# Products by seven in the down projection: fewer, later in their stages, and the turns before them on four banks

## Chip, cores and metric

The kernel runs on one core of one Trainium2 chip. The metric is the device time of an execution in microseconds; the time given for a kernel is the median of several runs. TensorE is called PE in the profile, VectorE DVE, ScalarE ACT, GpSimd POOL and SyncE SP.

## What is computed

One layer of an encoder for 256 tokens of width 2048 in float32. Attention in two kinds of windows comes first; then the gated MLP, which is where the change lies, and a gate by a second input:

```python
x = x + merged @ w_out[i]
hf = rms_norm(x, ffn_norm[i])
g = dwconv_centred(hf @ w_ffn_gate[i], conv_w[i], conv_b[i])
x = x + (jax.nn.gelu(g) * (hf @ w_ffn_up[i])) @ w_ffn_down[i]
gate_p = jax.nn.sigmoid(rms_norm(x, ple_norm[i]) @ w_ple_gate[i])
x = x + gate_p * (p[i] @ w_ple_proj[i])
...
return rms_norm(x, final_norm)
```

The MLP is 5632 wide (44 chunks of 128), with a convolution over three neighbouring tokens on the gate path.

## The kernel before

**Pieces.** All weights come from HBM as pieces of 128 x 2048 numbers (1 MB), in the order of use, into a ring of three buffers (`raw`, loads on SyncE's queue, L229). Each number is split into a high part (ScalarE, L249) and a low part (VectorE, L250). A product of two split operands is three matmuls (`thirds`, L350 to L352). The split units lie in a ring of six (`u`) and, for pieces by seven, a second ring of two (`v`), so VectorE and ScalarE can work ahead of TensorE by some three pieces.

**Plain pieces and pieces by seven.** In a `quad_stage` a piece holds two chunks of the contraction (a, b) by two column blocks of 512, and the tokens are two halves of 128. A plain piece (letter `s`) takes eight products, 24 matmuls of 512 columns, into the banks M2, M3, M4 and P22. A piece by seven (letter `S`) takes seven products, 21 matmuls, into M1, M7, M5, M6, M2, M3 and M4, by Winograd's form of Strassen's scheme. It asks for more elsewhere: VectorE forms differences of the weights in place (L242 to L244) and splits 3584 columns instead of 2048, and the moving side needs four sums of the activations of its two chunks, split too (`sums_of`, L821 to L827: four additions of 128 columns, a split of 512 on ScalarE and one on VectorE). Such a set of sums lies in one of five slots, tags 0 to 4. A set is made for a pair of chunks: pair 4 is chunks 8 and 9.

**Stages around the change.** The order is E0 to E5, F00, F01, E6 to E10, F10, F11, then pp0, pp1, G0, G2, G3. An E stage computes 512 columns of gate and of up for all tokens (8 pieces, pattern `ssssSsSs`). An F stage multiplies the activations of one half (24 or 20 chunks, so 12 or 10 pieces) with half of the columns of the down projection: F00 and F01 use groups 0 to 5, F10 and F11 groups 6 to 10. The letters of `DOWN` say which pieces of an F stage go by seven.

**What runs inside a stage.** Work on other engines is put at places (stage, piece, product) by `at` and issued when the loop gets there; the framework may still shift an instruction on its engine where its operands come late. At the start of a stage's last piece `row_sums` (L796 to L800) joins the banks of the products by seven: M1 by ScalarE, then M6, M7 and M5 on VectorE. As M2, M3, M4 and P22 end, `scaled` (L1021, L1022) finishes the rows of an E stage, and `residual` (L910 to L914) adds those of an F stage to the residual rows `xr`.

**Turns.** The rows of group g are turned to columns by TensorE in the next stage (`group_turns`, `turned`, L956: four transposes of 128 into a bank, copied out by ScalarE at L958): two calls for gate, two for up. The convolution and gelu (`mixer`, L965 to L973) and the product with up (`mixed`, L978 to L986) follow on VectorE and ScalarE, and `mixed` may make the set of sums at once (`held["early"]`). Sets that are not made there are made by `late` (L1016, then `sums_of`), which first adds the high and the low parts of the two chunks again. Four calls of `rows_pair` (L844, L447, L448) in F11 turn the first half of the new residual rows for the stage G0, and four more in pp0 the second half.

Of the kernel before, what the change touches and what calls it, by code (L numbers as in the profile page):

```python
# [90 lines left out]
NA = len(_JOBS)  # L91
ALT = "SsSsSsSs"
MLP = "ssssSsSs"
DOWN = ("SsSsSsSsSsss", "SsSsSsSsSs")
MLP_GROUPS = (range(0, 6), range(6, 11))
FIRST_GATES = "ssssSsSs"

# [1 line left out]
def _pieces():  # L99

    pieces, stages = [], {}

    def blocks(stage, items):
        stages[stage] = range(len(pieces), len(pieces) + len(items) // PIECE)
        for i in range(0, len(items), PIECE):
            pieces.append(("f", items[i:i + PIECE]))

    def quads(stage, n0, n1, pattern, k0=0):
        stages[stage] = range(len(pieces), len(pieces) + len(pattern))
        for i, c in enumerate(pattern):  # L110
            a, b = k0 + 2 * i, k0 + 2 * i + 1
            pieces.append((c, [(n0, a), (n1, a), (n1, b), (n0, b)]))

    def wide(stage, n, chunks):
        stages[stage] = range(len(pieces), len(pieces) + chunks // 4)
        for k in range(0, chunks, 4):
            pieces.append(("w", [(n, k + i) for i in range(4)]))

    a = [("w_in", k, j[2]) for k in range(KC) for j in _JOBS[:FIRST]]
    for _, _, n in _JOBS[FIRST:]:  # L120
        a += [("w_in", k, c) for k in range(KC) for c in (n if isinstance(n, tuple) else (n,))]
    blocks("A", a)
    for j in range(4):
        quads("B%d" % j, ("w_in", GA * P + j * WIDE), ("w_in", GB * P + j * WIDE), ALT if j else FIRST_GATES)
        wide("ba%d" % j, ("w_branch_a", j * WIDE), QH)
        wide("bb%d" % j, ("w_branch_b", j * WIDE), HG)
    for s in range(2):
        quads("D%d" % s, ("w_out", 2 * s * WIDE), ("w_out", (2 * s + 1) * WIDE), ALT)
    for half, groups in enumerate(MLP_GROUPS):
        for g in groups:  # L130
            quads("E%d" % g, ("w_ffn_gate", g * WIDE), ("w_ffn_up", g * WIDE), MLP)
        for s in range(2):
            quads("F%d%d" % (half, s), ("w_ffn_down", 2 * s * WIDE), ("w_ffn_down", (2 * s + 1) * WIDE),
                  DOWN[half], 4 * groups[0])
    for s in range(2):
        stages["pp%d" % s] = [len(pieces)]
        n0, n1 = ("w_ple_proj", 2 * s * WIDE), ("w_ple_proj", (2 * s + 1) * WIDE)
        pieces.append(("s", [(n0, 0), (n1, 0), (n1, 1), (n0, 1)]))
    quads("G0", ("w_ple_gate", 0), ("w_ple_gate", WIDE), ALT)
    for s in (2, 3):  # L140
        wide("G%d" % s, ("w_ple_gate", s * WIDE), KC)
    return pieces, stages


_PIECES, _STAGES = _pieces()
_NPIECES = len(_PIECES)

# [19 lines left out]
_LAST_OF = {u: o for u, o in _FBLOCKS}  # L167
_EARLY = [0] + list(np.cumsum([_LAST_OF[u] + 1 for u in range(40)]))
RINGS = {"u": 6, "v": 2}
HELD_TAGS = ({"act": (0, 1, 2, 3, 4), "next": (0, 1)}, {"act": (2, 3, 4, 0, 1), "next": (2, 3, 4, 0)})  # L170


@with_exitstack
def _encoder(ctx: ExitStack, tc, xt, pt, xrow, cols, gainrow, table, onehot, mask, ident_in, wts, out):
# [314 lines left out]
    due, rt, rc, held = {}, {}, {}, {}  # L489

    def at(i, f, *a):

        due.setdefault(i, []).append((f, a))
# [261 lines left out]
    for i, job in enumerate(_JOBS):  # L755
# [13 lines left out]
        if i == FIRST:  # L769
            for e in range(FIRST):  # L770
                late = max(e - KVH, 0)
# [38 lines left out]
    def quads(stage, moving, combos, finish):  # L810
        last = len(_STAGES[stage]) - 1
        row_sums(stage, last, finish)
        quad_stage(stage, moving, combos)
        run_due(stage, last, 8)
# [57 lines left out]
    for j in range(4):  # L872
# [15 lines left out]
        c = held["c"]  # L888
# [53 lines left out]
    mlp_pairs = [i for i, c in enumerate(MLP) if c == "S"]  # L942
# [7 lines left out]
    def turned(which, n, pair, c):  # L950

        p = bank(which, P, 2, T)
        for k in range(2):
            for t in range(2):
                first = n * WIDE + pair * T + k * P
                nc.tensor.transpose(p[:, k, t * P:(t + 1) * P], c[t][:, first:first + P], ident)  # L956
        u = held["tok"].tile([P, 2, T], F32, name="ut" if n else "gt", bufs=1 if n else 2)
        nc.scalar.activation(u, p, AF.Copy)  # L958
        return u

    def mixer(f, g):

        c = held["tok"].tile([P, 2, T], F32, name="cc")
        for k in range(2):
            nc.scalar.activation(c[:, k], g[:, k], AF.Identity, scale=tap(1, f + k), bias=tap(3, f + k))  # L965
            nc.vector.scalar_tensor_tensor(c[:, k, 1:], g[:, k, :-1], tap(0, f + k), c[:, k, 1:],
                                           op0=ALU.mult, op1=ALU.add)
            nc.vector.scalar_tensor_tensor(c[:, k, :-1], g[:, k, 1:], tap(2, f + k), c[:, k, :-1],
                                           op0=ALU.mult, op1=ALU.add)
        nc.scalar.activation(g, c, AF.Square, scale=math.sqrt(0.044715))  # L970
        nc.vector.scalar_tensor_tensor(g, g, 1.0, c, op0=ALU.add, op1=ALU.mult)
        nc.scalar.activation(g, g, AF.Tanh, scale=GELU_C)
        nc.vector.scalar_tensor_tensor(c, g, 1.0, c, op0=ALU.add, op1=ALU.mult)  # L973
        return c

    def mixed(k, c, u):

        nc.vector.scalar_tensor_tensor(u, u, 0.5, c, op0=ALU.mult, op1=ALU.mult)  # L978
        if 16 <= k < 20:
            for i in range(2):  # L980
                halves(activation_row(k + i), u[:, i])
        else:
            i = k // 20 * 2
            d = held["act"][i][:, k - 10 * i:k - 10 * i + 2]
            nc.scalar.activation(d[:, :, :T], u, AF.Copy)
            nc.vector.tensor_tensor(d[:, :, T:], u, d[:, :, :T].bitcast(F32), op=ALU.subtract)  # L986
        if k // 2 in held["early"]:
            combos["act", k // 2] = sums_of(u, held["early"][k // 2])

    def group_turns(half, g, down, c):  # L990

        k = 4 * (g - MLP_GROUPS[half][0])
        stage = "F%d0" % half if down else "E%d" % (g + 1)
        got = {}

        def gate(which, pair):
            got[pair] = turned(which, 0, pair, c)
            if pair == 0:
                got["c"] = mixer(4 * g, got[0])

        def up(which, pair):
            u = turned(which, 1, pair, c)
            mixed(k + 2 * pair, got["c"], u)
            if pair == 0:
                got["c"] = mixer(4 * g + 2, got[1])

        whens = ((0, 2), (0, 5), (1, 0), (1, 3)) if down else ((0, 3), (0, 6), (1, 1), (1, 5))
        for f, pair, which, when in zip((gate, gate, up, up), (0, 1, 0, 1), ("M1", "M5", "M6", "M7"), whens):
            at((stage, *when), f, "P22" if down else which, pair)

    def late(pair, tag):

# [19 lines left out]
        held["p"] = ph, pl  # L1032

    for half, groups in enumerate(MLP_GROUPS):
        pairs, tags = [i for i, c in enumerate(DOWN[half]) if c == "S"], HELD_TAGS[half]
        held["early"] = dict(zip(pairs, tags["act"][:3]))
        held["act"] = [big.tile([P, 16, 2 * T], FR, name="act", tag="R1"),
                       [big.tile([P, 2 * T], FR, name="act1", tag="yb%d" % i) for i in range(4)],
                       held["tok"].tile([P, 4, 2 * T], FR, name="act2")]
        for g in groups:  # L1040
            quads("E%d" % g, lambda k: hf[:, k, :], lambda i: combos["hf", i], scaled)
            group_turns(half, g, g == groups[-1], held["c"])
        for pair, tag in zip(pairs[3:], tags["act"][3:]):
            at(("F%d0" % half, pair - 4, 4), late, pair, tag)
        if half:
            at(("F10", 6, 0), load_last)
            at(("F10", 9, 0), split_last)
            held["ssq"] = sc.tile([P, 2, 2], F32, name="ssq", bufs=1)
        else:
            for pair, tag, when in zip(mlp_pairs, tags["next"], ((2, 4), (4, 4))):  # L1050
                at(("F01", *when), combine, "hf", hf, pair, tag)
        residual("F%d0" % half, 0, activation_row, "act", half)
        if half:
            pl = big.tile([P, KC, 2 * T], FR, name="pl", tag="R0")
            for pair, when in enumerate((("F11", 0, 6), ("F11", 1, 2), ("F11", 1, 5), ("F11", 2, 1))):
                at(when, rows_pair, "P22", pair, pl, 2)
            at(("F11", 2, 4), combine, "pl", pl, 0, tags["next"][0])
            at(("F11", 4, 4), combine, "pl", pl, 2, tags["next"][1])
        residual("F%d1" % half, 1, activation_row, "act", half)
# [52 lines left out]
    c = outputs()  # L1112
# [81 lines left out]
```

## Time and profile before

| what | value |
|---|---|
| median of 3 runs | 1469.82 us (1469.01 to 1470.96) |
| the profiled execution's own time | 1472.92 us |
| its span, first to last instruction | 1471.1 us |
| mean granted TensorE clock | 0.995 |
| ScalarE busy | 885.9 us (60%) |
| HBM read | 279.49 MB, 191 GB/s over the span |

Busy times are records that overlap on TensorE: the record of a matmul of 512 columns lasts 0.39 us, but the next one starts 0.23 later. So the space between starts is what counts there. In a row of a timeline the numbers are the start, the duration, the engine, the line, the operation and the tiles; in square brackets stands the idle time of the engine ahead of it and what ended that. In a row of a group, `x446 | 536.9, 1220 |` is the count, the busy time in us and the mean in ns.

### The profile page before, as it was taken

The page shows a single profiled execution, that of the slowest core. Times are in us where ns is not written, and L with a number is a line of the kernel's source. Part 1 is how long each engine was busy: PE and PEld are TensorE (multiplying, and loading weights), DVE is VectorE, ACT ScalarE, POOL GpSimd, SP SyncE. Part 2 cuts the span into 40 slices and gives each one's busy share as a digit, 9 for nine tenths or more (in the row PEclk, how much of TensorE's full clock was granted, in tenths as well). Part 3 has the DMA queues.
Part 4 walks back from the last instruction along what each step waited for, and adds up shares of the span by engine and source line. Part 5 has one row for each costly group of instructions (what it writes and reads, how often), then busy time and mean ns, then how long its engine had stood idle before and what let it go on. Part 6 is the DMA issues. An engine that isn't in the chain of part 4 may idle for free.

```text
span 1471.1 us, 18240 instructions
## 1 busy us (share of the span) xinstructions
PE 1449.0 (98%) x6892; PEld 1203.7 (82%) x6892; DVE 1292.3 (88%) x1720; ACT 885.9 (60%) x1188; POOL 4.9 (0%) x9
## 2 busy tenths in 40 slices
PE   9999999999999999999999999999999999989997
PEld 8888888888888888788888888788888878767786
DVE  7777764679998989999999999998899989999995
ACT  7555544445655655667666667554576766655663
POOL 0000000000000000000000000000000000000000
PEclk9999999999999999999999999999999999999998
DMA  9754445535555457454555444546535464345552
GB/s 324 256 203 143 168 163 183 175 120 208 217 188 212 172 200 273 163 193 176 225 200 200 170 174 172 216 185 246 211 136 203 177 228 173 145 157 218 200 206 111
DMA packets 46451, 282.80 MB, mean 192 GB/s; under 512 B 5076, under 2 KB 9812, under 8 KB 14108
## 3 DMA queue, kind: packets, MB, share of 16 engines
q1 hardware_dynamic: 45500, 280.46, 51.5%
q8 instruction: 54, 0.88, 0.2%
q10 hardware_dynamic: 864, 1.19, 0.2%
q14 instruction: 33, 0.27, 0.0%
HBM read 279.49 MB, written 2.14 MB: 191 GB/s over the span
## 4 chain that ended last, share of the span: by engine, by line
PE 88%; DVE 7%; ACT 2%; DMA 1%; issue 1%; POOL 0%; POOLq 0%; ACTq 0%; DVEq 0%
PE bank L351 22%; PE bank L352 22%; PE bank L350 22%; PE bank L293 7%; PE bank L300 4%; DVE ul L250 3%; PE bank L277 2%; PE bank L339 2%; PE bank L341 2%; PE bank L340 2%; DVE vl L250 1%; PE bank L956 1%; PE bank L278 1%; DMA raw<-in_wts 1%; ACT uh L249 1%
## 5 line engine op out<-in xcount | busy, mean ns | idle before, releaser
L249 ACT ACTIVATE uh<-raw 128x1024 fp32r<-128x1024 f32 (+2 forms) x518 | 507.5, 995 | 355.5 <-DMA raw<-in_wts 129.1
L250 DVE TENSOR_TENSOR ul<-raw,uh 128x1024 fp32r<-128x1024 f32 (+2 forms) x518 | 583.0, 1146 | 101.1 <-ACT uh L249 81.8
L350 PE MATMUL bank<-uh,hf 128*128 128x512 f32 x572 | 226.4, 396 | 0.6 <-DVE c L1021 0.6
L352 PE MATMUL bank<-uh,hf 128*128 128x512 f32 x572 | 223.3, 390 | 0.0
L351 PE MATMUL bank<-ul,hf 128*128 128x512 f32 x572 | 222.8, 389 | 0.0
L249 ACT ACTIVATE vh<-raw 128x1024 fp32r<-128x1024 f32 x136 | 143.1, 1056 | 59.1 <-DVE raw L242 33.2
L250 DVE TENSOR_TENSOR vl<-raw,vh 128x1024 fp32r<-128x1024 f32 x136 | 165.0, 1219 | 2.5 <-ACT vh L249 2.1
L352 PEld LDWEIGHTS bank<-uh,hf 128*128 128x128 f32 x572 | 107.3, 188 | 23.1
L350 PEld LDWEIGHTS bank<-uh,hf 128*128 128x128 f32 x572 | 107.4, 188 | 22.4 <-issue 1.3
L351 PEld LDWEIGHTS bank<-ul,hf 128*128 128x128 f32 x572 | 107.6, 188 | 21.2
L293 PE MATMUL bank<-hs,uh 128*128 128x512 f32 x432 | 103.6, 392 | 0.0
L350 PE MATMUL bank<-uh,act 128*128 128x512 f32 x232 | 89.9, 393 | 2.8 <-ACT uh L249 2.6
L293 PEld LDWEIGHTS bank<-hs,uh 128*128 128x128 f32 x432 | 79.5, 188 | 15.6
L351 PE MATMUL bank<-ul,act 128*128 128x512 f32 x232 | 90.5, 392 | 0.0
L352 PE MATMUL bank<-uh,act 128*128 128x512 f32 x232 | 90.1, 393 | 0.0
L350 PE MATMUL bank<-vh,S 128*128 128x512 f32 x204 | 79.7, 405 | 5.4 <-DVE c L797 3.1
L242 DVE TENSOR_TENSOR raw<-raw 128x1024 f32<-128x1024 f32 x68 | 82.9, 1220 | 0.5
L351 PE MATMUL bank<-vl,S 128*128 128x512 f32 x204 | 80.9, 396 | 0.6 <-DVE vl L250 0.6
L352 PE MATMUL bank<-vh,S 128*128 128x512 f32 x204 | 79.6, 393 | 0.0
L350 PE MATMUL bank<-uh,hs 128*128 128x512 f32 x172 | 67.3, 392 | 0.0
L352 PE MATMUL bank<-uh,hs 128*128 128x512 f32 x172 | 67.2, 391 | 0.0
L351 PE MATMUL bank<-ul,hs 128*128 128x512 f32 x172 | 67.1, 390 | 0.0
(254 smaller groups left out, 2565.7 us busy)
## 6 DMA issues: line engine op xcount, KB each, us to landing
raw<-in_wts SPq DMA_DIRECT2D x251, 1024.0 KB, 4.8
raw<-in_wts SPq DMA_DIRECT2D x12, 512.0 KB, 6.6
xr<-in_xrow SPq DMA_DIRECT2D x4, 512.0 KB, 8.1
x<-in_xt SPq DMA_DIRECT2D x13, 128.0 KB, 5.9
hb<-hold SPq DMA_DIRECT2D x3, 514.0 KB, 7.2
hb<-hold SPq DMA_DIRECT2D x2, 768.0 KB, 7.2
last<-in_gainrow SPq DMA_DIRECT2D x1, 1024.0 KB, 7.0
out<-xr SPq DMA_DIRECT2D x4, 256.0 KB, 2.6
```

The lines of the kernel that those rows point to most:

```text
L242: nc.vector.tensor_tensor(raw[:, :2 * WIDE], raw[:, WIDE:3 * WIDE], raw[:, :2 * WIDE], op=ALU.subtract)
L249: nc.scalar.activation(hi, src, AF.Copy)
L250: nc.vector.tensor_tensor(lo, src, hi.bitcast(F32), op=ALU.subtract)
L277: nc.tensor.matmul(acc, hi[:, w], m, start=first, stop=False, skip_group_check=True)
L293: nc.tensor.matmul(acc, weights(u)[0][:, o * P:(o + 1) * P], m, start=first, stop=False, skip_group_check=True)
L300: nc.tensor.matmul(acc[:, T:], weights(u)[1][:, o * P:(o + 1) * P], m[:, :T], start=False, stop=last, skip_group_check=True)
L339: nc.tensor.matmul(acc[:, :n * P], xh, hi, start=(k == 0), stop=False)
L340: nc.tensor.matmul(acc[:, :n * P], xh, lo, start=False, stop=False)
L341: nc.tensor.matmul(acc[:, :n * P], xl, hi, start=False, stop=(k == KC - 1))
L350: nc.tensor.matmul(acc, sh, wh, start=first, stop=False)
L351: nc.tensor.matmul(acc, sh, wl, start=False, stop=False)
L352: nc.tensor.matmul(acc, sl, wh, start=False, stop=last)
```

## The change

- `DOWN` has a pattern for each F stage: F00 four pieces by seven (pieces 4, 6, 8, 10), F01 five (0, 4, 6, 8, 10), F10 four (2, 4, 6, 8), F11 three (4, 6, 8). Before, each had five, at the even pieces from 0 to 8.
- The sets of sums of those pairs are made in `mixed`, where the activations arise. One set remains for `late`: pair 0 in half 0, made at piece 9 of F00 and used by F01's first piece. Slots and the two sets of `hf` made again in F01 move accordingly.
- The turns of a group stand at other places in the next stage: one or two products later in E stages, about three in F00, and in F10 at places of their own. Those of the last group of a half, which shared the bank P22, take M1, M5, M6 and M7 as the others do. So do the four turns of `rows_pair` in F11, at the places they had.

```diff
-DOWN = ("SsSsSsSsSsss", "SsSsSsSsSs")
+DOWN = (("ssssSsSsSsSs", "SsssSsSsSsSs"), ("ssSsSsSsSs", "ssssSsSsSs"))
...
-                  DOWN[half], 4 * groups[0])
+                  DOWN[half][s], 4 * groups[0])
...
-HELD_TAGS = ({"act": (0, 1, 2, 3, 4), "next": (0, 1)}, {"act": (2, 3, 4, 0, 1), "next": (2, 3, 4, 0)})
+HELD_TAGS = ({"act": {4: 0, 6: 1, 8: 2, 10: 3}, "next": (4, 0)},
+             {"act": {2: 1, 4: 2, 6: 3, 8: 4}, "next": (0, 1, 2, 3)})
...
-        whens = ((0, 2), (0, 5), (1, 0), (1, 3)) if down else ((0, 3), (0, 6), (1, 1), (1, 5))
+        whens = ((0, 5), (1, 0), (1, 3), (1, 6)) if stage != "F10" else ((0, 4), (0, 6), (1, 0), (1, 2))
         for f, pair, which, when in zip((gate, gate, up, up), (0, 1, 0, 1), ("M1", "M5", "M6", "M7"), whens):
-            at((stage, *when), f, "P22" if down else which, pair)
+            at((stage, *when), f, which, pair)
...
-        pairs, tags = [i for i, c in enumerate(DOWN[half]) if c == "S"], HELD_TAGS[half]
-        held["early"] = dict(zip(pairs, tags["act"][:3]))
+        tags = HELD_TAGS[half]
+        held["early"] = tags["act"]
...
-        for pair, tag in zip(pairs[3:], tags["act"][3:]):
-            at(("F%d0" % half, pair - 4, 4), late, pair, tag)
...
-            for pair, tag, when in zip(mlp_pairs, tags["next"], ((2, 4), (4, 4))):
+            at(("F00", 9, 4), late, 0, 4)
+            for pair, tag, when in zip(mlp_pairs, tags["next"], ((2, 4), (6, 4))):
                 at(("F01", *when), combine, "hf", hf, pair, tag)
...
-            for pair, when in enumerate((("F11", 0, 6), ("F11", 1, 2), ("F11", 1, 5), ("F11", 2, 1))):
-                at(when, rows_pair, "P22", pair, pl, 2)
+            for pair, (which, when) in enumerate((("M1", (0, 6)), ("M5", (1, 2)), ("M6", (1, 5)), ("M7", (2, 1)))):
+                at(("F11", *when), rows_pair, which, pair, pl, 2)
```

## Prediction

> **What bounds the kernel now.** I read the page first, then busy time by stage, then TensorE's rows where a stage is longer than its matmuls, then what VectorE and ScalarE did there.
>
> ```profile
> span 1471.1 us, 18240 instructions
> PE 1449.0 (98%) x6892; PEld 1203.7 (82%) x6892; DVE 1292.3 (88%) x1720; ACT 885.9 (60%) x1188; POOL 4.9 (0%) x9
> ```
>
> TensorE looks full, but matmul records overlap, so 98% hides short stalls. The table by stage shows them better. Its rows are, in order, E3, E5, F00, F01, E6, E10, F10, F11 and G0 (a stage runs from its first product to the next stage's first).
>
> ```profile
> core 0: us, PE busy (x) PEld busy (x) DVE busy (x) ACT busy (x) POOL busy (x), PEclk, DMA share, GB/s
> 761.34:806.18 44.84, 44.43 (x202) 36.51 (x203) 42.67 (x57) 31.24 (x42) 0.00 (x0) 1.00 0.52 189
> 850.28:894.37 44.09, 44.09 (x203) 36.47 (x202) 41.37 (x52) 30.62 (x42) 0.00 (x0) 1.00 0.45 161
> 894.37:961.82 67.45, 65.72 (x290) 51.86 (x289) 65.87 (x91) 43.39 (x56) 0.00 (x0) 1.00 0.49 186
> 961.82:1023.70 61.88, 61.88 (x274) 51.24 (x273) 58.34 (x70) 31.73 (x36) 0.00 (x0) 1.00 0.59 227
> 1023.70:1065.86 42.16, 42.16 (x187) 34.91 (x186) 34.15 (x36) 21.38 (x24) 0.00 (x0) 1.00 0.55 209
> 1198.91:1243.75 44.84, 44.43 (x202) 36.50 (x203) 42.12 (x52) 31.75 (x42) 0.00 (x0) 1.00 0.45 166
> 1243.75:1298.93 55.18, 54.48 (x243) 42.93 (x241) 54.82 (x81) 37.79 (x53) 0.00 (x0) 1.00 0.51 191
> 1298.93:1360.87 61.94, 56.50 (x238) 44.73 (x237) 58.93 (x77) 33.80 (x43) 0.00 (x0) 0.94 0.46 172
> 1373.64:1417.74 44.10, 42.38 (x185) 33.79 (x184) 42.98 (x61) 26.43 (x37) 1.07 (x1) 1.00 0.57 218
> ```
>
> A piece by seven products is 21 matmuls of 512 columns, a plain one 24. F01 holds 5x21 + 7x24 = 273 and no transposes, and took 61.88: 0.2267 us each. E6 confirms it (2x21 + 6x24 = 186; 42.16 / 186 = 0.2267). E5 has the same 186 and 16 transposes of a group's turns: 44.09 - 42.17 = 1.92, or 0.12 a transpose with its interruption. What exceeds this is stall:
> - F00: 67.45 - 61.88 - 1.92 = 3.65.
> - F10: 225 matmuls, 51.00; 55.18 - 51.00 - 1.92 = 2.26.
> - F11: 225 and 12 transposes; 61.94 - 51.00 - 1.44 = 9.50.
> - E3 and E10: 44.84 - 44.09 = 0.75 each.
> - G0: 180 matmuls and 4 transposes; 44.10 - 40.80 - 0.48 = 2.82.
>
> F00 and F10 are the stages where VectorE has no idle time (65.87 of 67.45, 54.82 of 55.18): it bounds them. F11 begins with what F10 left undone. Its first piece in TensorE's rows, then VectorE's:
>
> ```profile
> 1301.13 0.50 PE L350 MATMUL bank<-uh,act 128*128 128x512 f32 x1 [1.36 <-ACT uh L249]
> 1304.72 0.77 PE L350 MATMUL bank<-vh,S 128*128 128x512 f32 x1 [3.09 <-DVE c L797]
> 1305.29 0.63 PE L351 MATMUL bank<-vl,S 128*128 128x512 f32 x1
> 1305.71 0.63 PE L352 MATMUL bank<-vh,S 128*128 128x512 f32 x1
> ...
> 1309.55 0.55 PE L352 MATMUL bank<-uh,S 128*128 128x512 f32 x1
> 1309.94 0.39 PE L350 MATMUL bank<-uh,act 128*128 128x512 f32 x1
> ```
> ```profile
> 1301.63 1.22 DVE L250 TENSOR_TENSOR ul<-raw,uh 128x1024 fp32r<-128x1024 f32 x1
> 1302.76 1.21 DVE L250 TENSOR_TENSOR vl<-raw,vh 128x1024 fp32r<-128x1024 f32 x1
> 1303.90 0.68 DVE L797 TENSOR_TENSOR c<-bank,c 128x512 f32<-128x512 f32 x1
> 1304.50 0.67 DVE L910 TENSOR_TENSOR xr<-xr,bank 128x512 f32<-128x512 f32 x1
> ```
>
> F11 begins with a product by seven, which needs the banks M1, M7, M5 and M6 at once. They still hold F10's sums, whose first reader on VectorE (L797) stands behind weight splits and starts at 1303.90. TensorE waits 1.36 and 3.09. Then 11 matmuls come 0.43 apart instead of 0.23, at a granted clock that is 0.94 over the stage: 11 x 0.2 = 2.2 more. That is 7.4 of F11's 9.50 with the small gaps.
>
> [...]
>
> **The change part by part.**
>
> *Fewer pieces by seven.* 5+5+5+5 become 4+5+4+3. Four pieces go from 21 matmuls to 24: 12 x 0.2267 = +2.72 us on TensorE, certain: F00 276, F01 273, F10 228, F11 231. What each saves on VectorE comes from these groups:
>
> ```profile
> L250 DVE TENSOR_TENSOR ul<-raw,uh 128x1024 fp32r<-128x1024 f32 x446 | 536.9, 1220 | 84.3 <-ACT uh L249 65.8 <-PE bank L300 15.0 <-issue 1.9
> L250 DVE TENSOR_TENSOR vl<-raw,vh 128x1024 fp32r<-128x1024 f32 x136 | 165.0, 1219 | 2.5 <-ACT vh L249 2.1
> L242 DVE TENSOR_TENSOR raw<-raw 128x1024 f32<-128x1024 f32 x68 | 82.9, 1220 | 0.5
> L250 DVE TENSOR_TENSOR ul<-raw,uh 128x512 fp32r<-128x512 f32 x70 | 48.0, 686 | 12.3 <-ACT uh L249 11.4
> L243 DVE TENSOR_TENSOR raw<-raw 128x512 f32<-128x512 f32 x68 | 46.6, 685 | 0.5
> L244 DVE TENSOR_TENSOR raw<-raw 128x512 f32<-128x512 f32 x68 | 46.6, 685 | 0.4
> L827 DVE TENSOR_TENSOR S<-cmb,S 128x512 fp32r<-128x512 f32 x26 | 17.8, 684 | 0.1
> L821 DVE TENSOR_TENSOR cmb<-ut 128x128 f32<-128x128 f32 x26 | 7.4, 286 | 0.2
> L1016 DVE TENSOR_TENSOR ut<-act 128x256 f32<-128x256 f32 x8 | 3.2, 418 | 0.0
> ```
>
> By seven: 1.22 + 2 x 0.685 of differences, then splits 0.686 + 3 x 1.22. Plain: 2 x 1.22. The difference by durations is 4.5; the VectorE rows above start 1.13 and 0.60 apart, which makes it 4.1 of its time. A set of sums costs 0.684 + 4 x 0.286 = 1.8, and 2 x 0.42 more where it is made late: half 0 keeps five sets with one late instead of two, half 1 has four, none late, instead of five with two late. ScalarE, busy 43.39 of F00's 67.45, has room either way.
>
> Against TensorE's new need: F00 65.87 - 4.1 - 0.8 = 61.0 of 62.57 + 1.92 = 64.49 (95%, E5's share, which has no stall). F10, with about 5 us of its work that spilled into F11, needs some 60 now. It loses 4.1 and 2 x 0.84 + 1.8 = 3.5 of sums, since one of its two late sets is gone and the other is made at once: 52.4 of 53.60. That is full, but it enters with the weights of two pieces split ahead. F11 loses the spill and 2 x 4.1: 58.93 - 5 - 8.2 = 46 of 54.28. So I take the stalls of all three as gone: F00 64.49 (-2.96), F10 53.60 (-1.58), F11 54.28 (-7.66), the added matmuls included. What is late next is the bank M2, with which plain first pieces begin.
>
> *Turns placed later, on four banks.* E stages take them one or two products later (6 x 0.2267 = 1.36), F00 about three; F10 moves the first two later and the last one earlier.
>
> ```profile
> 1198.91 0.47 PE L350 MATMUL bank<-uh,hf 128*128 128x512 f32 x1 [0.55 <-DVE c L1021]
> 1201.75 0.55 PE L956 MATMUL bank<-ident,c 128*128 128x128 f32 x3 [0.41 <-ACT c L1022]
> 1371.27 1.15 PE L844 MATMUL bank<-ident,xr 128*128 128x128 f32 x9
> 1378.24 0.47 PE L350 MATMUL bank<-uh,pl 128*128 128x512 f32 x1 [0.79 <-DVE pl L448]
> ```
>
> In E10 the first turn waited 0.41 for scaled rows, 0.6 with the interrupted stream; E3 had the same. 1.36 later the rows are there: 2 x 0.6 = -1.2. In F00 and F10 the one bank cost little, since their 16 transposes show no long wait. In F11 the fourth pair's turn shares its bank with a running accumulation and slipped out of the stage: the 9 transposes at 1371 are part of 20 where four pairs need 16. On M7 it stays in F11: its 0.48 moves there (counted above), and G0 loses 0.48 and part of 2.82 of stall, one part of which is the 0.79 for L448. No row shows that cover, so between 0 and 2.82 I take 1.0, near the 0.79.
>
> *Sums made once, in the mixing.* ScalarE's split of a late sum stood in front of weights:
>
> ```profile
> 927.17 0.63 ACT L826 ACTIVATE S<-cmb 128x512 fp32r<-128x512 f32 x1 [5.11 <-DVE cmb L824]
> 930.81 0.73 PE L350 MATMUL bank<-uh,act 128*128 128x512 f32 x2 [1.21 <-ACT uh L249]
> ```
>
> That is F00's stall, counted already. New stalls: F11 and F00 begin plain and may wait for M2 as E10 did (0.55), and the one late sum left may hold ScalarE. Between 0 and 3.6 (F00's whole stall) I take +1.0, nearest the 0.55. The slots of the moved sets (tag 4 after E5, tag 0 after F01's fifth piece) are free pieces before their writers come, so I cost those waits at nothing; were one late, VectorE's weight splits queued behind it would pay. Pieces, their number and their loads on SyncE's queue stay as they are.
>
> **Sum.** -2.96 - 1.58 - 7.66 - 1.2 - 0.48 - 1.0 + 1.0 = -13.9. The profiled execution took 1472.92 (span 1471.1), so it would take 1459.0. The median of the runs, 1469.82, is 3.1 below it, and becomes 1455.9. A measurement tells some 0.2%, 2.9 us, from no change.
>
> **Rivals.**
> 1. *The stalls shrink only in part.* F10 stays full (52.4 of 53.60), so F11 starts late again. If 40% of 15.4 us of stalls stays, 6.2 is given back: 1462.1. For it: VectorE's need comes in lumps of a group's mixing. Against: F11 no longer asks for M1 first.
> 2. *The remaining late sum blocks ScalarE before F01*, as at 927: 3.6 back, 1459.5. [...]
> 3. *Slower: the later turns starve E stages.* VectorE idles 44.09 - 41.37 = 2.72 in E5. If the turns' 1.36 is lost for it and both following pieces by seven wait that long, each of the nine E stages with turns pays 2.72: 24.5 - 13.9 = +10.6, 1480. It decides from 13.9 / 9 = 1.5 a stage. Against: the idle time covers one such shift.
> 4. *The places do not bind.* The order on the engines is not the written one (the slipped turn shows it); if the turns run where they ran, the 1.2, 0.48 and 1.0 stay: 1458.6.
>
> **How the numbers follow.** Forecast 60%, rival 1 17%, rival 2 7%, rival 4 9%, rival 3 7%. The range goes from 1453.0 (all of G0's 2.82 and no new stall: 1.8 and 1.0 less) to 1462.0, rival 1. Faster by over 0.2% takes all but rival 3 and the worst of rival 1: 0.89; same 0.05; slower 0.06.
>
> **What would show it.** Right: F00 near 64.5, F10 53.6, F11 54.3 with a clock of 1.00, no wait on L797 over 1 us, E3 and E10 at 44.1, all 16 turns of the first four pairs in F11. Wrong: F stages over these by more than 2 us, E stages above 45, or VectorE idle in E5 over 3 us while TensorE waits on its splits.

## The result, and the profile after

The changed kernel takes 1460.01 us (median of 6 runs, 1459.24 to 1460.69). The kernel before took 1470.94 in the 6 runs beside it (1469.01 to 1471.51). The ratio is 0.9929, with a 95% interval from 0.9916 to 0.9941: 10.9 us faster. The forecast time was 1455.9, with a range from 1453.0 to 1462.0. The profiled execution took 1460.40, with a span of 1458.6.

The table of stages, with the columns shown before, has these rows for the changed kernel: E3, F00, F01, E10, F10, F11 and G0.

```profile
core 0: us, PE busy (x) PEld busy (x) DVE busy (x) ACT busy (x) POOL busy (x), PEclk, DMA share, GB/s
762.33:806.49 44.16, 44.16 (x203) 36.49 (x203) 41.79 (x56) 30.51 (x41) 0.00 (x0) 1.00 0.52 191
894.88:960.50 65.62, 65.01 (x294) 53.22 (x292) 62.31 (x82) 43.81 (x56) 0.00 (x0) 1.00 0.49 179
960.50:1022.70 62.20, 62.20 (x275) 51.15 (x273) 59.37 (x73) 32.86 (x36) 0.00 (x0) 1.00 0.62 229
1197.66:1242.83 45.17, 44.36 (x202) 36.40 (x203) 41.70 (x56) 30.14 (x42) 0.00 (x0) 1.00 0.50 187
1242.83:1296.95 54.12, 54.05 (x245) 44.29 (x245) 53.97 (x72) 37.69 (x51) 0.00 (x0) 1.00 0.52 199
1296.95:1351.25 54.30, 54.30 (x249) 44.87 (x247) 52.02 (x69) 31.57 (x42) 0.00 (x0) 1.00 0.55 199
1364.04:1405.24 41.20, 41.20 (x181) 33.53 (x180) 40.47 (x56) 24.48 (x30) 1.07 (x1) 1.00 0.64 241
```

F11 is now as long as TensorE's records in it (54.30 of 54.30), at a clock of 1.00. F00 and F10 came down too; they are 1.1 and 0.5 us longer than their matmuls and turns. G0 gave 2.9 us, and nothing in it was edited. From E1 to F11, TensorE's rows hold four waits of more than 0.15 us. Three are for the bank M2, at the first product of E3 (0.45), E10 (0.38) and F10 (0.81); the fourth is in F00's seventh piece, for a weight split. The two longest:

```profile
1242.83 0.47 PE L351 MATMUL bank<-uh,act 128*128 128x512 f32 x1 [0.81 <-DVE c L1022]
...
932.03 0.50 PE L352 MATMUL bank<-vl,S 128*128 128x512 f32 x1 [0.61 <-DVE vl L251]
```

(Lines of the changed kernel stand one later: L1021 is L1022, L250 is L251.)

| stretch | before | after | difference | predicted |
|---|---|---|---|---|
| E1 to E5 and E7 to E10 | 399.35 | 399.33 | 0.0 | -1.2 |
| F00 | 67.45 | 65.62 | -1.8 | -3.0 |
| F01 | 61.88 | 62.20 | +0.3 | 0 |
| F10 | 55.18 | 54.12 | -1.1 | -1.6 |
| F11 | 61.94 | 54.30 | -7.6 | -7.7 |
| pp0, pp1, G0 | 56.87 | 53.99 | -2.9 | -1.5 |
| new stalls, in no stage | | | | +1.0 |

(A wait for a stage's first product is counted to the stage before it, so F10's 0.81 is in E10.) The rows add up to -13.1. The spans differ by 12.5, since stages ahead of E1 took 0.6 longer, which the edit does not touch.

### The profile page after: what moved, and what is told of

The parts are those of the page before. It is cut to its first block, busy times and chain, and to the rows that moved or that the text cites. A ratio compares the mean times of both kernels' runs of the same rounds, so it can differ in the third digit from the quotient of the medians.

```text
span 1458.6 us, 18224 instructions
## 1 busy us (share of the span) xinstructions
PE 1444.6 (99%) x6904; PEld 1205.6 (83%) x6904; DVE 1273.4 (87%) x1689; ACT 880.7 (60%) x1179; POOL 4.8 (0%) x9
## 4 chain that ended last, share of the span: by engine, by line
PE 83%; DVE 11%; DMA 2%; issue 2%; ACT 2%; POOLq 0%; POOL 0%; DVEq 0%; SPq 0%; ACTq 0%
PE bank L351 21%; PE bank L353 20%; PE bank L352 20%; PE bank L294 7%; DVE ul L251 4%; PE bank L301 4%; DMA raw<-in_wts 2%; PE bank L340 2%; PE bank L342 2%; PE bank L341 2%; PE bank L278 2%; DVE vl L251 1%; PE bank L279 1%; DVE raw L243 1%; PE bank L845 1%
## 5 line engine op out<-in xcount | busy, mean ns | idle before, releaser
L250 ACT ACTIVATE uh<-raw 128x1024 fp32r<-128x1024 f32 (+2 forms) x518 | 507.8, 999 | 346.7 <-DMA raw<-in_wts 119.7
L251 DVE TENSOR_TENSOR ul<-raw,uh 128x1024 fp32r<-128x1024 f32 (+2 forms) x518 | 584.0, 1149 | 100.0 <-ACT uh L250 80.9
L250 ACT ACTIVATE vh<-raw 128x1024 fp32r<-128x1024 f32 x128 | 134.5, 1057 | 65.6 <-DVE raw L243 29.4
L251 DVE TENSOR_TENSOR vl<-raw,vh 128x1024 fp32r<-128x1024 f32 x128 | 155.0, 1218 | 0.9 <-ACT vh L250 0.5
L351 PE MATMUL bank<-uh,act 128*128 128x512 f32 x256 | 100.9, 394 | 0.8 <-DVE c L1022 0.8
L353 PE MATMUL bank<-uh,act 128*128 128x512 f32 x256 | 100.0, 391 | 0.0
L352 PE MATMUL bank<-ul,act 128*128 128x512 f32 x256 | 99.7, 389 | 0.0
L243 DVE TENSOR_TENSOR raw<-raw 128x1024 f32<-128x1024 f32 x64 | 78.0, 1219 | 0.6
L352 PE MATMUL bank<-vl,S 128*128 128x512 f32 x192 | 75.4, 392 | 0.6 <-DVE vl L251 0.6
L351 PE MATMUL bank<-vh,S 128*128 128x512 f32 x192 | 75.7, 398 | 0.1
L353 PE MATMUL bank<-vh,S 128*128 128x512 f32 x192 | 74.3, 390 | 0.0
```

The costliest lines, as they stand in the source:

```text
L243: nc.vector.tensor_tensor(raw[:, :2 * WIDE], raw[:, WIDE:3 * WIDE], raw[:, :2 * WIDE], op=ALU.subtract)
L250: nc.scalar.activation(hi, src, AF.Copy)
L251: nc.vector.tensor_tensor(lo, src, hi.bitcast(F32), op=ALU.subtract)
L351: nc.tensor.matmul(acc, sh, wh, start=first, stop=False)
L352: nc.tensor.matmul(acc, sh, wl, start=False, stop=False)
L353: nc.tensor.matmul(acc, sl, wh, start=False, stop=last)
```

## The experiments

The notation is as in the diff above. Each kernel ran in turn with the kernel before, as a rule five times (ten times in experiment 2, four times for the second kernel of experiment 9).

**1. F11 alone, in the kernel before.** The first two experiments ask why F11 stalled for 9.5 us.

```diff
-DOWN = ("SsSsSsSsSsss", "SsSsSsSsSs")
+DOWN = (("SsSsSsSsSsss",) * 2, ("SsSsSsSsSs", "ssssSsSsSs"))
...
-            for pair, when in enumerate((("F11", 0, 6), ("F11", 1, 2), ("F11", 1, 5), ("F11", 2, 1))):
-                at(when, rows_pair, "P22", pair, pl, 2)
+            for pair, (which, when) in enumerate((("M1", (0, 6)), ("M5", (1, 2)), ("M6", (1, 5)), ("M7", (2, 1)))):
+                at(("F11", *when), rows_pair, which, pair, pl, 2)
```

> The kernel before, in which F11 alone begins with four plain pieces (three by seven instead of five) and turns its four pairs on M1, M5, M6 and M7. F00, F01 and F10 stay as before, so F10 leaves as much VectorE work undone as before. Theory A (F11's 9.5 us of stall are F10's undone VectorE work): the undone work stays, F11's first products wait for M2 in place of M1, F11 is 58 us or more, and the time 1465 or more. Theory B (the stall is that a piece by seven asks for M1, M7, M5 and M6 at once): F11 is near 54.3, G0 near 41.2 as in the changed kernel, and the time 1460 to 1462. F10 stays near 55.2 in both.

It took 1464.38 us, 0.9963 of before (0.9950 to 0.9975). The stages F10, F11 and G0, and TensorE's row between the first two:

```profile
1241.17:1299.22 58.05, 54.72 (x243) 42.72 (x241) 57.77 (x84) 37.98 (x52) 0.00 (x0) 1.00 0.51 194
1299.22:1354.38 55.16, 54.68 (x247) 44.93 (x248) 51.37 (x68) 31.66 (x42) 0.00 (x0) 1.00 0.55 200
1367.87:1409.24 41.37, 41.21 (x182) 33.69 (x181) 40.64 (x56) 24.39 (x30) 1.07 (x1) 1.00 0.66 249
```
```profile
1299.22 0.50 PE L350 MATMUL bank<-uh,act 128*128 128x512 f32 x1 [2.63 <-DVE xr L910]
```

The wait of 2.63 ends with F11's first product, so the table counts it to F10. It is the undone work of theory A: M2, in place of M1, comes free late. But it is one wait instead of two, and the clock stays at 1.00. With the wait F11 is 57.8, just under theory A's 58, and the time is just under its 1465; without it F11 is 55.2, and G0 is where theory B has it. So the truth lies between the two.

**2. F11 alone as before, in the changed kernel.**

```diff
-        ... ("ssSsSsSsSs", "ssssSsSsSs"))
+        ... ("ssSsSsSsSs", "SsSsSsSsSs"))
...
+            at(("F10", 5, 4), late, 0, 0)
...
-            ... ((("M1", (0, 6)), ("M5", (1, 2)), ("M6", (1, 5)), ("M7", (2, 1)))):
+            ... ((("P22", (0, 6)), ("P22", (1, 2)), ("P22", (1, 5)), ("P22", (2, 1)))):
```

> The changed kernel with F11 as before: five pieces by seven from its first piece on, turns on P22; the sums of pair 0 are made late in F10. Theory A (undone work of F10, which is now gone): F11 is 51.0 of matmuls + 1.4 of turns + at most 1.5 of waiting, 54 or less, with a clock of 1.00; with 2.9 given back in G0 for the slipped turn the time is about 1462.5. Theory B (the form with which F11 begins): a wait on L798 of 3 us or more, a slower clock and F11 of 58 to 62, so a time of 1467 to 1470.

It took 1467.79 us, 0.9978 of before (0.9969 to 0.9987). F10, F11 and G0, and the first waits in F11:

```profile
1243.15:1297.36 54.21, 54.12 (x244) 44.18 (x245) 54.17 (x77) 38.67 (x53) 0.00 (x0) 1.00 0.47 180
1297.36:1354.80 57.44, 54.15 (x239) 42.95 (x238) 56.82 (x75) 32.75 (x42) 0.00 (x0) 1.00 0.49 184
1367.53:1411.64 44.11, 42.52 (x186) 33.76 (x185) 43.26 (x62) 26.80 (x37) 1.06 (x1) 1.00 0.57 222
```
```profile
1299.36 0.50 PE L351 MATMUL bank<-uh,act 128*128 128x512 f32 x1 [1.16 <-ACT uh L250]
1301.01 0.50 PE L351 MATMUL bank<-vh,S 128*128 128x512 f32 x1 [1.15 <-DVE c L798]
```

The two waits are those of before, 1.36 and 3.09, made smaller. F10 and F11 together took 117.12 before, 113.21 in the first experiment, 111.65 here and 108.42 in the changed kernel. Relieving F10 is worth 4.8 to 5.5 us, and beginning F11 plainly, with two pieces by seven fewer, 3.2 to 3.9. Neither theory holds alone: theory B's time came, but not its wait of 3 us or its slower clock. The shares add up, and F10's is the greater.

**3. The fourth turn on P22 again.**

```diff
-            ... ("M6", (1, 5)), ("M7", (2, 1)))):
+            ... ("M6", (1, 5)), ("P22", (2, 1)))):
```

> The changed kernel with one edit: the fourth turn of the residual rows in F11 is put on P22 again. Theory: the turn slips out of F11 as before, F11 loses 0.5 us, G0 goes from 41.2 back towards 44.1, and the time is 1462.4. Rival: G0 became shorter because VectorE arrives there with less undone work, and the turn does not matter: G0 stays under 42 and the time at 1460.0.

It took 1460.71 us, 0.9930 of before (0.9918 to 0.9942), which cannot be told from the changed kernel. F11, then pp0 with pp1, then G0, and the last turns:

```profile
1295.26:1349.07 53.81, 53.81 (x245) 44.48 (x244) 50.93 (x67) 30.58 (x40) 0.00 (x0) 1.00 0.55 198
1349.07:1362.77 13.70, 13.56 (x69) 10.82 (x68) 13.49 (x20) 13.07 (x25) 0.00 (x0) 1.00 0.28 98
1362.77:1404.10 41.33, 41.20 (x181) 33.68 (x180) 40.60 (x56) 24.46 (x31) 1.07 (x1) 1.00 0.62 245
```
```profile
1357.69 1.58 PE L845 MATMUL bank<-ident,xr 128*128 128x128 f32 x13
```

The turn did slip: its transposes come after F11, among the 13 at 1357.69. G0 stays short all the same. The slip costs 0.4 net (13.70 against 12.79, and F11 0.49 less). So the slip of this turn is not what G0's gain comes from, and the rival stands.

**4. Four pieces by seven in F11.**

```diff
-        ... ("ssSsSsSsSs", "ssssSsSsSs"))
+        ... ("ssSsSsSsSs", "ssSsSsSsSs"))
...
-            ... ((("M1", (0, 6)), ("M5", (1, 2)), ("M6", (1, 5)), ("M7", (2, 1)))):
+            ... ((("M1", (0, 6)), ("M5", (1, 0)), ("M6", (1, 2)), ("M7", (1, 5)))):
```

> The changed kernel with four pieces by seven in F11 (2, 4, 6, 8) instead of three, and its turns up to one product earlier. TensorE needs 0.7 us less, VectorE 4.1 more. Theory (what VectorE saves in F11 is spent on working ahead, and shortens G0): G0 goes from 41.2 to 42.5 or more, the time stays at 1460 to 1462. Rival (F11 has room for it, as predicted by its 46 of 54 us): F11 53.6, G0 41.2, time 1459.3.

It took 1460.20 us, 0.9931 of before (0.9919 to 0.9943). F11 and G0:

```profile
1296.89:1350.60 53.71, 53.71 (x245) 44.29 (x244) 53.21 (x71) 32.59 (x43) 0.00 (x0) 1.00 0.51 189
1363.40:1405.05 41.65, 41.52 (x181) 33.49 (x180) 40.84 (x59) 25.10 (x34) 1.07 (x1) 1.00 0.61 230
```

F11 gains 0.6, as the rival had it, G0 loses 0.45, and the time stays. G0's 41.65 is under the 42.5 that the theory set, but goes its way a little. VectorE's busy time rose by 1.2 in F11, not by the 4.1 that the added piece asks for, so it did less of something else there. Over the kernels shown, busy times of 50.93 to 53.21 in F11 go with 41.20 to 41.65 in G0, though not in order; the second experiment's 56.82 and the 58.93 of before go with 44.11 and 44.10. That fits an engine that spends what it need not do in F11 on working ahead for G0. It is argued, not shown: no run varies that lead by itself, and both kernels with the long G0 also turn all four pairs in F11 on P22.

**5. The E stages' turns at their old places.**

```diff
+        if stage[0] == "E":
+            whens = ((0, 3), (0, 6), (1, 1), (1, 5))
```

> The changed kernel with the turns in the E stages at the places of before; F00 and F10 keep the new ones. Theory (the later turns save the waits for scaled rows in two stages): 1461.2, with the sum of E1 to E5 and E7 to E10 1.2 us longer. Rival (the places only move the waits from one stage to another): 1460.0 within 0.4. Second rival (the later turns cost VectorE time): 1459.0 or less.

It took 1461.69 us, 0.9937 of before (0.9923 to 0.9950), an interval that overlaps the changed kernel's. E3, E9 and E10, and E3's wait (in this kernel L1022 is L1025):

```profile
761.92:806.76 44.84, 44.43 (x203) 36.52 (x203) 42.69 (x57) 31.10 (x42) 0.00 (x0) 1.00 0.52 188
1153.96:1198.06 44.10, 44.10 (x204) 36.48 (x203) 41.16 (x55) 29.43 (x40) 0.00 (x0) 1.00 0.51 187
1198.06:1242.73 44.67, 44.37 (x204) 36.44 (x203) 41.76 (x56) 30.26 (x41) 0.00 (x0) 1.00 0.52 191
```
```profile
764.76 0.55 PE L957 MATMUL bank<-ident,c 128*128 128x128 f32 x3 [0.41 <-ACT c L1025]
```

The 0.41 in E3 comes back, so the later place does remove it. But E10 is 0.5 shorter than in the changed kernel, and the nine E stages take 398.80, where the theory had them 1.2 longer than the changed kernel's 399.33. The gain of a stage is lost in another, as the first rival has it. The rival's time did not come: the median is 1.7 over the changed kernel's. In the profile the excess lies outside the E stages (pp0 with pp1 takes 14.29 for 12.79), and whether it means anything, the intervals do not say.

**6. Two sets of sums made late again.**

```diff
-HELD_TAGS = ({"act": {4: 0, 6: 1, 8: 2, 10: 3}, ...
-             {"act": {2: 1, 4: 2, 6: 3, 8: 4}, ...
+HELD_TAGS = ({"act": {4: 0, 6: 1, 8: 2}, ...
+             {"act": {2: 1, 4: 2, 6: 3}, ...
...
+            at(("F10", 4, 4), late, 8, 4)
...
+            at(("F00", 6, 4), late, 10, 3)
```

> The changed kernel with two of its sets of sums made late again: pair 10 at the seventh piece of F00 and pair 8 at the fifth piece of F10. Each costs VectorE 0.84 us more, and a split on ScalarE that waits for VectorE. Theory (VectorE and ScalarE are full in F00 and F10, so a late set is paid for by TensorE): F00 and F10 1 to 2 us longer each, 1462 to 1464. Rival (it costs no more than can be hidden): 1460.0 within 0.5.

It took 1461.83 us, 0.9938 of before (0.9925 to 0.9950): 1 to 2 us over the changed kernel, within what the intervals leave open. F00 and F10 are not longer (65.07 and 54.11); F01 is 63.24 and F11 55.10, 1.0 and 0.8 over the changed kernel. F01's is one wait, in its first piece:

```profile
961.68 0.47 PE L351 MATMUL bank<-vh,S 128*128 128x512 f32 x1 [1.07 <-DVE c L798]
```

If the sets have a price, it shows a stage later than the theory put it.

**7. Five pieces by seven in F00.**

```diff
-DOWN = (("ssssSsSsSsSs", ...
+DOWN = (("ssSsSsSsSsSs", ...
...
+        if stage == "F00":
+            whens = ((0, 4), (0, 6), (1, 0), (1, 2))
...
+        if not half:
+            at(("E5", 7, 4), late, 2, 4)
         for g in groups:
```

> The changed kernel with five pieces by seven in F00 (pieces 2, 4, 6, 8, 10) instead of four; the sums of pair 2 are made late, at the end of E5; F00's turns stand where F10 has them. TensorE needs 0.7 us less, VectorE 6.7 more (4.1 for the piece, 2.6 for the set). Theory (the number of pieces by seven bounds F00 through VectorE): F00 67 or more, time 1461.5 to 1464. Rival (that they begin after two plain pieces is what counts): F00 65 and time 1459.3.

It took 1465.56 us, 0.9955 of before (0.9942 to 0.9969): 5.5 slower than the changed kernel. Four of the five executions took 1464.31 to 1465.91 at a mean granted clock of 0.996 or 0.997, the fifth 1461.97 at 0.998. F00 and F01, and F01's start:

```profile
893.92:959.04 65.12, 64.25 (x290) 52.69 (x290) 63.22 (x87) 43.04 (x57) 0.00 (x0) 1.00 0.48 178
959.04:1025.62 66.58, 64.01 (x275) 52.35 (x273) 63.64 (x77) 34.52 (x38) 0.00 (x0) 0.97 0.59 215
```
```profile
960.71 0.50 PE L351 MATMUL bank<-vh,S 128*128 128x512 f32 x1 [0.84 <-ACT vh L250]
962.95 0.80 PE L352 MATMUL bank<-vl,S 128*128 128x512 f32 x1 [1.74 <-DVE vl L251]
963.54 0.63 PE L353 MATMUL bank<-vh,S 128*128 128x512 f32 x1
963.97 0.63 PE L351 MATMUL bank<-vh,S 128*128 128x512 f32 x1
```

The median is 1.6 over the theory's range, and the loss is not where the theory put it. F00 itself is 0.5 shorter, as the rival had it, and F01 pays 4.4, with a slow clock again (0.97 over the stage). F01 was not edited. Late pieces alone do not help: with five of them the debt is paid where the next stage begins by seven. This is how F10 and F11 stood to each other before. The edit does three things, and no run separates the piece, its set made late and the places of the turns.

**8. F01 like F00, with no late set at all.**

```diff
-        ... "SsssSsSsSsSs"), ...
+        ... "ssssSsSsSsSs"), ...
...
-            at(("F00", 9, 4), late, 0, 4)
```

> The changed kernel with F01 as F00 (four pieces by seven, the first at piece 4), so that the late set of pair 0 is gone. TensorE needs 0.7 us more in F01. Theory (F00's wait of 0.8 at its piece 6 is for the late set, which VectorE takes there already): F00 from 65.6 to 64.6, F01's 0.3 gone, together 0.6 less: 1459.4. Rival (the wait has another cause): F00 65.6 and the time 1460.5.

It took 1459.88 us, 0.9926 of before (0.9913 to 0.9938): no different from the changed kernel. F00 is 65.95, and its wait of 0.6 in the seventh piece is still there, so the late set is not its cause. F01 is 63.25, of which its 276 matmuls take 62.57, so F01's 0.3 did not go either. Rows of the changed kernel ahead of F00's wait suggest another cause. They are VectorE's and SyncE's (with what SyncE waited for from 905 to 921 us, in total, times and longest), then ScalarE's and VectorE's:

```profile
918.40 1.22 DVE L251 TENSOR_TENSOR vl<-raw,vh 128x1024 fp32r<-128x1024 f32 x1
919.65 0.33 SPq L230 DMA_DIRECT2D raw<-in_wts  x1
```
```profile
SPq L230 <- DVE vl L251: 14.8, 1, 14.8
```
```profile
925.65 1.06 ACT L250 ACTIVATE uh<-raw 128x1024 fp32r<-128x1024 f32 x1 [4.76 <-DMA raw<-in_wts]
```
```profile
926.74 1.22 DVE L251 TENSOR_TENSOR ul<-raw,uh 128x1024 fp32r<-128x1024 f32 x1 [0.97 <-ACT uh L250]
```

SyncE had waited 14.8 us for a buffer of the ring of three, until VectorE, with rows of the mixing between its splits, had read it out at 919.62. The load then came late, ScalarE and VectorE idled for it, and the split that TensorE wanted stood behind that piece's. So the late load is VectorE's lag again, by way of the buffers. This is read from the rows; no run varies the buffers, so it stays open.

**9. More pieces by seven where VectorE has time: E6.** E6 has no turns, and VectorE worked 34 of its 42 us.

```diff
-            quads("E%d" % g, ..., MLP)
+            quads("E%d" % g, ..., MLP if g != 6 else "ssSsSsSs")
...
+            at(("F01", 8, 4), combine, "hf", hf, 2, 1)
```

> The changed kernel with one piece by seven more in E6 (2, 4, 6 instead of 4, 6); the sums of its pair are made in F01. E6 has no turns, and VectorE is busy 34 of its 42 us. TensorE needs 0.7 us less, VectorE 4.1 + 2.4 more. Theory (an added piece by seven is free where VectorE has idle time, and only there): E6 41.5 without waits, E7 unchanged, 0.7 less than the changed kernel. Rival (the debt appears in E7, as F10's does in F11): E6 41.5, but E7 0.5 to 2 longer, and the time the same or longer.

The second kernel has "SsSsSsSs" there, and the sets of the pairs 0 and 2 made in F01's ninth and eleventh pieces.

> The changed kernel with two pieces by seven more in E6 (0, 2, 4, 6). TensorE needs 1.4 us less, VectorE 13 more, which is over E6's 8 us of idle time by 5. Theory: what exceeds the idle time comes out of the lead of VectorE, and is paid for in E6 or E7: E6 40.8 or more, E7 1 to 3 longer, 0.5 to 2 us slower than with one more. Rival (F01's idle time and the lead of two pieces carry it): 1.4 less than the changed kernel.

They took 1459.83 (0.9929, 0.9915 to 0.9943) and 1458.34 us (0.9916, 0.9903 to 0.9930). E6 of the changed kernel, then E6 and E7 of the second:

```profile
1022.70:1064.86 42.16, 42.16 (x188) 34.91 (x186) 34.17 (x36) 21.38 (x24) 0.00 (x0) 1.00 0.54 205
1022.22:1063.11 40.89, 40.89 (x182) 33.65 (x181) 40.68 (x47) 21.48 (x24) 0.00 (x0) 1.00 0.58 219
1063.11:1107.26 44.15, 44.15 (x204) 36.43 (x202) 41.75 (x53) 30.15 (x40) 0.00 (x0) 1.00 0.55 203
```

E6 went from 42.16 to 41.51 and 40.89, and E7, 44.07 in the changed kernel, stayed at 44.07 and 44.15. The theory for the second kernel was wrong, and its rival right: VectorE's busy time grew by 6.5 us in E6 and by 2.6 in F01 (61.96 for 59.37), and neither F01 (62.17) nor E7 is longer for it. (F00, which the edit does not reach, is 66.65 and 66.53 in these two profiles, 0.9 to 1.0 over the changed kernel.) With "SsSsSsSs" the kernel has the lowest median of the study.

**10. The changed kernel again.**

> The changed kernel again, to stand beside the others on the same chip: 1460.0 within 1.0; the stages of its profile within 0.3 of the first, except F00, whose wait at piece 6 may differ by 1.

It took 1460.58 us, 0.9930 of before (0.9918 to 0.9943). F00 is 65.65, F10 54.08, F11 54.30 and G0 41.21. E2 differs by 0.6 (44.10 against 44.71), more than the 0.3 expected. So differences of half a microsecond in one E stage mean nothing, and the nine E stages cannot show the 1.2 that was forecast either. The second kernel of experiment 9 is 2.2 us below this one, with intervals that overlap; the 1.2 of it that E6 and E7 hold is what its edit explains, and the profiled executions of the two (1459.48 and 1459.37) do not differ.

## Why the prediction was right, and where it was not

**The mechanism held.** VectorE bounded F00 and F10 (before, it was busy 65.87 of 67.45 and 54.82 of 55.18 us), and fewer pieces by seven relieve it. Experiment 7 shows it from the other side: one piece more, with its set made late and the turns' places that go with it, costs 5.5 us, though TensorE needs 0.7 less. Of this the slow clock is some 1.7, an estimate from 3.41 us at half clock in F01. The added matmuls came as counted: F11 is 231 x 0.2267 + 1.92 = 54.29, measured 54.30, and the wait on L797 (3.09 before) and the slow clock (0.94 over F11 before, 1.00 now) are gone. The forecast of -7.66 for F11 takes the slow clock's 2.2 as gone with the waits. F11 now runs at 1.00, with no wait of more than 0.15 us. At what length of wait the 2.2 goes, no run shows: the clock stayed at 1.00 through 2.63 in experiment 1 and fell in a wait of 1.74 in experiment 7.

**F11's stall has two causes**, as the prediction had it without their shares: F10's debt (4.8 to 5.5 us) and the start by seven with its two further pieces (3.2 to 3.9).

**The size was off.** Forecast were 13.9 us, measured 10.9; the time of 1460.01 is inside the range. The profiled execution of before, against which the sum was made, lies 2.0 above the median of before over the six runs, the one after 0.4 above its own. So 12.5 in the profiles is 10.9 in the medians: 1.6 of the gap of 3.0 comes from there, 0.6 from the stages ahead of E1, and 0.8 from terms of the sum. That these leave only 0.8 is luck in part: the stages that gave less than forecast miss by 3.2 together, and G0's larger gain and the new stalls, which the rows hold already, give back 2.4.
- *F00, -1.8 for -3.0.* The step "95%, E5's share, which has no stall" failed (E5's own is 94%, 41.37 of 44.09). VectorE is at 62.31 of 65.62, but a wait of 0.6 in the seventh piece remains, which is not the late set's. A mean share leaves room for a split that stands behind a late load, and for a load that VectorE let start late.
- *E stages, 0.0 for -1.2.* "1.36 later the rows are there" was right for E3's turn, and the wait for M2 took its place: E3 begins with 0.45 of it, F10 with 0.81, and E10 is 0.3 longer than before. In experiment 10, the same kernel, the nine stages take 398.61, so the 0.0 is uncertain by 0.7.
- *G0 and its neighbours, -2.9 for -1.5.* The step "G0 loses 0.48 and part of 2.82 of stall" blamed the slipped turn. Experiment 3 puts the turn back, and G0 stays at 41.33. Of the 2.82 of stall 0.4 is left. That it went because F11 no longer leaves VectorE behind fits experiments 1, 2 and 4, but is not shown by itself.
- *VectorE's need in F11, 46 of 54.28*, measured 52.02. The estimate stopped at the stage's own work; by experiment 4, an engine with room seems to work ahead for the next stage, so its busy time falls by less than its need.
- *New stalls, +1.0.* M2 was the right bank, but F00 and F11, for which the term was made, show none of it; it is F10's 0.81 and E3's 0.45. That the late set held TensorE, no row shows.

**The rivals.** By the time alone, 1460.01 is nearer to the first (1462.1), the second (1459.5) and the fourth (1458.6) than to the forecast of 1455.9, which also started from a median of before that was 1.1 lower; the stages tell them apart. The first, in part: F10 stays full (53.97 of 54.12) but F11 does not start late, and what F00 keeps is of its kind, if the rows in experiment 8 are read rightly: VectorE's mixing comes in lumps and delays a load. The second, the late set before F01: F01 is 0.3 longer, not 3.6. The third, slower E stages: they are not. The fourth, places that do not bind: true in sum for the E stages, for another reason, and the slipped turn was indeed worth nothing; but the turns do run at other places, as E3 shows.

## What to carry to other kernels

Here the debts of VectorE, which works ahead, were paid a stage later (F10's cost F11 4.8 to 5.5 us): look for the cause of a stall at a stage's start in the stage before, and count what a relieved engine does ahead for the next. The exchange between work on TensorE and on VectorE is best set stage by stage, by the idle time of each: here fewer pieces by seven were faster in full stages, and two more of them took 1.3 us off E6, which had 8 us of idle time, with no price in the stages beside it. Forecast the median from several runs, not from one profiled execution alone.

## What the runs showed of the hardware

In these traces the slow clock does not go by the length of a single wait. The granted clock is the third number from the end; before, then in experiment 7:

```profile
1301.00:1303.04 2.04, 0.50 (x1) 0.19 (x1) 2.04 (x3) 1.97 (x3) 0.00 (x0) 1.00 0.00 0
1303.04:1309.86 6.82, 5.14 (x12) 4.10 (x13) 6.82 (x11) 1.06 (x1) 0.00 (x0) 0.50 0.80 308
```
```profile
959.50:962.89 3.39, 0.88 (x3) 0.19 (x1) 3.39 (x4) 2.98 (x4) 0.00 (x0) 1.00 0.13 14
962.90:966.31 3.41, 3.36 (x8) 2.69 (x9) 3.41 (x6) 0.00 (x0) 0.00 (x0) 0.50 0.82 332
```

Before, the clock falls to half inside the wait of 3.09, and is low for 6.82 us. In experiment 7 it falls just ahead of the end of a wait of 1.74, which one matmul parts from a wait of 0.84. A wait of 2.63 in experiment 1 brought no fall, and two of 1.16 and 1.15 in experiment 2 brought none either.

What makes the clock fall, the runs do not show. Executions of one kernel differ in their mean clock: in experiment 1 one of five took 1468.57 us at 0.996, the others 1464.03 to 1465.77 at 0.997 or 0.998.
